# Attention: a tile's normalization issued ahead of the next tile's scores on VectorE, and the adaLN slabs spread otherwise over the rounds

## The chip, the cores and the metric

One core of one Trainium2 chip. The time is the device time of one execution in microseconds (us), from the first to the last instruction of the program with what lies around them; several executions are timed and the median is given. The trace is of one execution taken by the hardware profiler. Engines: PE is TensorE (PEld its weight loads), ACT ScalarE, DVE VectorE, POOL GpSimd, SP the engine that issues the transfers. Each runs its own instructions in the order in which the program issues them, and waits for others by semaphores.

## The reference

Two trunk layers over 128 context tokens and 512 latent tokens, width 1024, in float32. Each layer: half a SwiGLU, a mixer, half a SwiGLU, each behind an RMS norm that is scaled and shifted by vectors from the condition ("adaLN": nine vectors of 1024 for each layer, `silu(cond) @ w_ada + b_ada`). The mixer of layer 0 is what matters here:

```
proj = h @ w_in ; q, k, v, xb, gb = split(proj)
q = rms_norm(q) / 8 ; k = rms_norm(k)                  # over each head's 64 channels
latent: s = [q . k(8 x 16 neighbourhood) + bias | q . k_cached]   # 8 heads
context: s = q . k
p = softmax(s) ; o = p . v
y = concat(o, rglru(xb, gb)) @ w_out ; x = x + gate * y
```

## The kernel before, in words

Channels lie on the 128 partitions, tokens along the free dimension: 640 tokens in two halves of 320. Every float32 product is made of three passes over a high and a low part of each operand, so every weight, 128 x 1024 at a time (512 KB), is loaded, copied to its high part on ScalarE (`whi`, L176), and its low part is subtracted (`wlo`, L181), here on GpSimd while the attention runs.

The work is written out by hand in program order, with `manual_schedule`; nothing is reordered. What decides the order around the change:

- **The load list.** `add_w` and `add_slab` append weights and slabs to one list, `self.loads`. A *slab* is one 128 x 1024 piece of `w_ada`; eight of them make an adaLN vector. `load()` (its transfer is L139, on SP) takes the head of the list whenever a load buffer is free in program order, and stops where none is. Weights and slabs of the mixer share three load buffers, `self.buffers(self.const, None, 3, 5)`: three for loads (`st`), five pairs for split weights (`whi`, `wlo`). For the mixer's end the list holds the output weight `w_out_ab` number 0, then slabs up to 79, then `w_out_ab` 1 to 7.
- **`fill(n)`** uses n slabs: eight small matmul records each (`ada`, L327), then the slab's buffer is free and `load()` is called. After the eighth slab of a vector ScalarE evacuates the sums (`adaev`), and at the next vector's first slab `ada_end` turns them (`adaT`) and adds the bias on VectorE.
- **`prep(upto, 1)`** first calls `flush()`, which issues the low part of a weight begun earlier and frees its load buffer, then `load()`, then issues at most one new split (the high part), if that weight's load has been issued.

```
def split_later(self, it, hi, lo, src, then=None):
    self.nc.scalar.activation(out=hi, in_=src, func=AF.Copy)
    self.lows.append((it, hi, lo, src, then))     # low part and free_raw come with the next flush
```

The attention works on 20 tiles: four channel groups c of two heads, and for each five tiles j of 128 queries (j = 0 to 3 latent with 384 keys, j = 4 context with 128). It is a software pipeline over 23 rounds s:

- `A(s)`: scores on TensorE (`S`, L1262), bias and minimum on VectorE from PSUM (two instructions, L1268), two exponentials with their sums on ScalarE (L1271);
- `N(s)`: reciprocal of the sums and two scalings of the exponentials on VectorE (L1277, L1279);
- `B(s)`: transposes on TensorE (`PT`, L1288) and one copy out on ScalarE (`pt`, L1291);
- `C(s)`: products with v on TensorE (`o`, `op`, L1301); after j = 3 and j = 4 the high part on ScalarE (`hh`, L1307) and the low part on VectorE (`hl`, L1308).

Where a group begins, `vtr` transposes v (`vT`, L1243). GpSimd prepares the next group's bias (`nb`, L1233) as the tiles before it let go of the old one. A round before the change is B(s-2), one slab, A(s) with these, N(s-1), a piece of other work in the first rounds (`early`), one slab, C(s-3), `prep`. 36 slabs (44 to 79) are left when the attention begins, three of them loaded.

After the attention comes the output projection (`out_last`, its sums `pd`), which needs the adaLN vector of the gate, and uses `w_out_ab` 0 to 7 in order.

Of the kernel before, what the change touches and what calls it, by code (L numbers as in the profile page):

```python
# [13 lines left out]
PSUM = bass.MemoryType.PSUM  # L14

P = 128
# [16 lines left out]
class Item:  # L33
    """weights of one product: their loads, the steps that split them, what the steps made"""
# [7 lines left out]
class Kern:  # L42
# [21 lines left out]
    def buffers(self, pool, phase, n_st, n_w):  # L64
        """buffers for weights: as loaded, and split; those of a phase serve its weights only"""
        for j in range(n_st):
            self.st_free.append((pool.tile([P, 1024], F32, name=f"st{j}"), phase))
        for j in range(n_w):
            self.w_free.append((pool.tile([P, 1024], F32R, name=f"whi{j}"),
                                pool.tile([P, 1024], F32R, name=f"wlo{j}"), phase))  # L70
# [14 lines left out]
    def slab_pool(self, st, upto, bufs=2):  # L85
        """weights of the adaLN vectors: slabs up to this one are used in the phase"""
        self.slab_p = st.enter_context(self.tc.tile_pool(name="slab", bufs=bufs))
        self.s_dma = self.s_use
        self.s_end, self.s_bufs = upto, bufs

    def psum(self, pairs):
        """PSUM of a phase: six single banks or three pairs"""
        if self.ps_pairs is pairs:
            return
        self.ps_st.close()
        self.ps_pairs = pairs
        ps = self.ps_st.enter_context(self.tc.tile_pool(name="ps", bufs=3 if pairs else 6, space=PSUM))
        if pairs:
            self.pair = lambda name: ps.tile([P, 2, 512], F32, tag="mm", name=name)
            self.bank = lambda name: self.pair(name)[:, 0, :]  # L100
        else:
            self.bank = lambda name: ps.tile([P, 512], F32, tag="mm", name=name)
# [48 lines left out]
    def prep(self, upto, most=99):  # L151
        """steps for the items up to this one, as far as there are buffers"""
        self.flush()
        self.load()
        while self.steps and most:
            it, fn, need = self.steps[0]
            if it.idx >= min(upto, self.limit) or len(it.raw) < len(it.src) and fn in (self.split_w, self.quad_a, self.fold_a):
                return
            w = None
            if need:  # L160
                w = self.pick(self.w_free if need == 1 else self.s1_free, it.slots)
                if w is None:
                    return
            self.steps.pop(0)
            self.flush()
            fn(it, w)
            most -= 1
            self.load()
# [5 lines left out]
    def split_later(self, it, hi, lo, src, then=None):  # L174
        """the low part comes with the next step"""
        self.nc.scalar.activation(out=hi, in_=src, func=AF.Copy)  # L176
        self.lows.append((it, hi, lo, src, then))
# [18 lines left out]
    def fold_a(self, it, w):  # L196
        """rows m and -m: sum and difference"""
# [12 lines left out]
    # a pair of units as a 2 x 2 matrix (unit, half of the rows): the seven left factors of Strassen and Winograd  # L210
# [59 lines left out]
    def done(self, most=99):  # L270
        """the oldest unit in use is no longer needed"""
# [3 lines left out]
    def mm3(self, out, w, ks, xs, first=True, last=True):  # L275
        """out (+)= W^T X in three passes; w: (hi, lo) as [P, k, 128], xs: k -> (hi, lo)"""
# [8 lines left out]
    def mm_side(self, outs, ws, h, lag=0):  # L285
        """products of several units with half h, chunk after chunk as the norm gives them; the last two unit by unit
        lag: chunks by which the last unit stays behind"""
# [57 lines left out]
    def ada_end(self):  # L345
        """the finished vector, channels on partitions"""
# [28 lines left out]
    def parts(self, h):  # L375
        """pieces of a token half with one condition: (column slice, condition)"""
# [20 lines left out]
    def norm_s(self, h, bank=None):  # L397
        """sums of squares, tokens on partitions"""
# [6 lines left out]
    def norm_a(self, h):  # L405
        """rsqrt(mean(x^2) + eps)"""
# [4 lines left out]
    def rsqrt(self, ps, n=3):  # L411
        """rsqrt(mean(x^2) + eps) of n columns of sums"""
# [3 lines left out]
        # the exponent halved on the bits, then Newton's steps  # L416
# [21 lines left out]
    def T_pool(self, ks=range(4)):  # L438
        """right factors of Strassen and Winograd beside the parts of h"""
# [9 lines left out]
    def norm_r(self):  # L449
        """the factors of the tokens on all partitions"""  # L450
# [6 lines left out]
    def norm_high(self, h, l, i, c, r, keep):  # L457
        """h = rms_norm(x) g (1 + scale) + shift and its high part
        keep: for the products of a SwiGLU"""
# [24 lines left out]
    def direct(self, l, i, h, c, keep):  # L484
        """the high part comes without the sum of product and shift"""
# [19 lines left out]
    def norm_steps(self, h, l, i, keep=False):  # L505
        """a step for each chunk, low parts one step behind"""
# [17 lines left out]
    def t_sums(self, k, b12, b22):  # L524
        """T1 = B12 - B11, T2 = B22 - T1, T3 = B22 - B12, T4 = B21 - T2"""
# [21 lines left out]
    # slabs of a SwiGLU: after chunks of the first units, and after each quad  # L547
# [5 lines left out]
    def plan_ffn(self, l, n, s):  # L553
        """weights of a SwiGLU in the order of their use; s: the first slab, returns the next"""
# [36 lines left out]
    def ffn(self, l, i, after, mid=iter(()), late=None):  # L591
        """after(h, c): what follows the last update of chunk c, half h; mid: steps of other work, one in each quad;
        late: what follows the last quad"""
# [14 lines left out]
    def ffn_start(self, evac):  # L608
        """the first products of all: the first two vectors of adaLN come chunk by chunk, the norm and the products follow"""
# [7 lines left out]
        def ada(c):  # L617
            """the vectors' values for a chunk, four sums in groups of columns"""
# [178 lines left out]
    def down_last(self, fs, gate, after):  # L797
        """the last product before a norm: half 0 is through while four chunks of half 1 remain
        the first sums wait for the last chunk of the inner width"""
# [20 lines left out]
    def quad(self, f, fills, begin=False):  # L820
        """gate and up of a chunk, both halves of the tokens, in seven products
        M1 = A11 B11, M2 = A12 B21, M3 = S4 B22, M4 = A22 T4, M5 = S1 T1, M6 = S2 T2, M7 = S3 T3;
        C11 = M1 + M2, U2 = M1 + M6, C12 = U2 + M5 + M3, C21 = U2 + M7 + M4, C22 = U2 + M7 + M5"""
# [73 lines left out]
    def out_last(self, xs, gate, after):  # L897
        """the last product before a norm: half 0 is through while four chunks of half 1 remain"""
# [32 lines left out]
    def mix_setup(self):  # L931
        """parameters of the mixer, log_sigmoid(lambda)"""
# [13 lines left out]
        # y = |lam|, w = exp(-y) by halving steps and a series  # L946
# [17 lines left out]
        # log1p(w) = 2 artanh(w / (2 + w))  # L964
# [11 lines left out]
        # -2 log_sigmoid = 2 (2 artanh) - 2 min(lam, 0)  # L976
# [24 lines left out]
    def lru(self, c, xc, gel):  # L1001
        nc, lp = self.nc, self.lp
        n = 644
# [19 lines left out]
        for d in range(2):  # L1023
            # exp(-z) and t = tanh(z / 2): 1 - a = t (1 + a), 1 - a^2 = t (1 + a)^2
# [28 lines left out]
    def qk_norm(self, which, c, ps):  # L1053
        """RMS norm over each head's 64 channels; q also gets -1/8"""
# [47 lines left out]
    def mixer0(self, after):  # L1102
        nc, tc = self.nc, self.tc
        self.bg, self.fg = [], []
        with ExitStack() as st:
# [18 lines left out]
            with ExitStack() as s2:  # L1124
# [60 lines left out]
                def early():  # L1185
                    """work that the first tiles of the attention cover"""
# [41 lines left out]
    def bias(self, c, v):  # L1228
        """mask less position bias of a variant of the windows' columns"""
# [6 lines left out]
    def attention(self, early):  # L1236
# [82 lines left out]
        n = len(tiles)  # L1319
        for s in range(n + 3):  # L1320
            if 0 <= s - 2 < n:
                B(*tiles[s - 2])
            self.fill(min(1, 80 - self.s_use))
# [12 lines left out]
            if 0 <= s - 1 < n:  # L1336
                N(*tiles[s - 1])
            next(early, None)
            self.fill(min(1, 80 - self.s_use))
# [12 lines left out]
    def fourier_const(self):  # L1352
        """the DFT matrices in the place of the right factors, a step for each piece"""
# [18 lines left out]
        def steps():  # L1372
# [9 lines left out]
            # the shift times the root of the number of tokens, by chunk in the group, group, condition  # L1382
# [10 lines left out]
    def scaled(self, h, c):  # L1393
        """x g (1 + scale) in parts; the factors of the tokens follow the channels' transform"""
# [12 lines left out]
    def fourier_front(self, const):  # L1407
        """what follows the updates before the transform"""
# [25 lines left out]
    def tok_rest(self):  # L1434
        """factors of the other tokens; the third tile has the end of half 0 and the start of half 1"""
# [8 lines left out]
    def fourier(self, after):  # L1444
        nc, tc = self.nc, self.tc
        NP, NQ, MP, MQ = self.NP, self.NQ, self.MP, self.MQ
        with ExitStack() as st:
# [6 lines left out]
            with ExitStack() as s2:  # L1454
# [11 lines left out]
                def chan(k, g):  # L1466
                    """the channels' transform: token tile k, group g"""
# [9 lines left out]
                def chan_out(k, g):  # L1477
                    """times the factors of the tokens, in parts"""
# [26 lines left out]
                # the shift's part, the same for all tokens  # L1505
# [25 lines left out]
                def pos(r):  # L1531
                    """rows r: cosines of group r, 4 the Nyquist channels, 5 + g sines of group g"""
# [9 lines left out]
                    def shift(q):  # L1542
                        """the shift stays at the first position"""
# [18 lines left out]
            with ExitStack() as s2:  # L1562
# [14 lines left out]
                for c in range(KD):  # L1577
# [17 lines left out]
                    # token n has the sum, the one as far from the end the difference  # L1595
# [16 lines left out]
    def run(self, stop=99):  # L1612
        nc, a = self.nc, self.a
        const = self.const
        with self.tc.manual_schedule():
# [29 lines left out]
            for n in range(KD):  # L1645
                if n == 1:
                    for i in range(s, 80):
                        self.add_slab(i, None)
# [21 lines left out]
            def after(l, i, first=4, per=3, keep=True):  # L1670
                """the next norm: half 0 while the last products of half 1 run"""
# [49 lines left out]
def pack(inp):  # L1721
    """lays the inputs out; no arithmetic"""
# [9 lines left out]
    # the first two vectors by chunks of channels  # L1732
# [47 lines left out]
    # DFT matrices: channels (columns: cosines 0..127, the first halved, cosine 128, sines 1..127) and positions  # L1780
# [37 lines left out]
```

## Time and profile before

| | us |
|---|---|
| median of 3 runs | 2305.5 (2305.37 to 2310.3) |
| span of the profiled execution | 2305.0 |
| busy in it: PE / DVE / ACT / POOL | 2224.0 / 1554.8 / 990.7 / 954.9 |
| first slab of the attention to its end, 689.06 to 778.50 | 89.44 |
| busy there: PE / DVE / ACT / POOL | 72.44 / 46.46 / 53.77 / 29.35 |

The profile gives no time of its own for the profiled execution beside its span. Rows of the timeline give start, duration, engine, line, operation, tiles written and read with their shapes and the count of merged instructions; in brackets stand the idle time before it and who ended it. Rows of the chain of waits give start, duration and what the end waited for at that moment. The busy time of PE is the union of modelled spans, so it is not the same as PE at its peak.

### The profile page before, as it was taken

To read this page: it belongs to the slowest core of one execution; us is meant where nothing else is said; L and a number is where in the kernel's file an instruction comes from. 1 tells how busy PE (TensorE), PEld (TensorE's weight loads), DVE (VectorE), ACT (ScalarE), POOL (GpSimd) and SP (SyncE) were. 2 spreads that over 40 slices of the span, in tenths; PEclk is the share of its full clock that TensorE was granted. 3 is DMA by queue.
4 is the path that set the end of the run, shared out by engine and by line. 5 is a ranking of instruction groups with operands and counts; after the bars stand their busy time and mean duration, and the time that the engine had idled before them with its cause. 6 is when DMAs were issued, how large, how long until landed. Compare 5 with 4: busy or idle time off the path is not lost.

```text
span 2305.0 us, 39901 instructions
## 1 busy us (share of the span) xinstructions
PE 2224.0 (96%) x15534; PEld 2110.0 (92%) x15534; DVE 1554.8 (67%) x2871; ACT 990.7 (43%) x1780; POOL 954.9 (41%) x856
## 2 busy tenths in 40 slices
PE   7999999999998899999999999999999989999999
PEld 5889999999994788999999889999999979999999
DVE  6676677666865368666666786666667786666665
ACT  4433333347855435333333453333335553333332
POOL 2444444440023235444444454444443645444441
PEclk9999999999999999999999999999999999999999
DMA  7333333321228424333322243332332322222221
GB/s 278 113 111 105 105 107 107 115 74 56 73 71 267 131 83 137 110 101 110 106 91 97 75 155 120 110 97 96 103 117 62 128 85 83 83 83 83 83 89 57
DMA packets 75316, 245.44 MB, mean 106 GB/s; under 512 B 8756, under 2 KB 12996, under 8 KB 75128
## 3 DMA queue, kind: packets, MB, share of 16 engines
q1 hardware_dynamic: 74168, 241.28, 31.7%
q8 instruction: 123, 2.02, 0.4%
q10 hardware_dynamic: 864, 1.38, 0.2%
q14 instruction: 65, 0.53, 0.1%
q0 software_dynamic: 96, 0.22, 0.0%
HBM read 239.71 MB, written 3.15 MB: 105 GB/s over the span
## 4 chain that ended last, share of the span: by engine, by line
PE 79%; DVE 13%; ACT 4%; issue 2%; POOL 2%; DMA 1%; ACTq 0%; DVEq 0%; SPq 0%; POOLq 0%
PE q L282 40%; PE pd L282 26%; PE pj L282 5%; DVE wlo L181 2%; PE ada L327 2%; DVE tl L172 1%; PE pg L282 1%; PE gt L1014 1%; PE pos L1549 1%; DVE x L381 1%; PE S L1262 1%; DVE y L473 1%; DVE sx L1268 1%; PE PT L1288 1%; DMA st<-w_ada 1%
## 5 line engine op out<-in xcount | busy, mean ns | idle before, releaser
L181 DVE TENSOR_TENSOR wlo<-st,whi 128x1024 fp32r<-128x1024 f32 (+2 forms) x401 | 498.4, 1254 | 11.1 <-ACT whi L176 10.2
L176 ACT ACTIVATE whi<-st 128x1024 fp32r<-128x1024 f32 (+2 forms) x405 | 401.2, 992 | 233.0 <-POOL st L232 139.3
L282 PE MATMUL pd<-g,whi 128*128 128x320 f32 x1536 | 347.0, 310 | 4.3 <-DVE u L825 2.3
L381 DVE SCALAR_TENSOR_TENSOR x<-pd,mods,x 128x128 f32<-128x128 f32 (+2 forms) x696 | 265.0, 433 | 111.7 <-PE pd L282 111.2
L282 PE MATMUL q<-hh,wlo 128*128 128x320 f32 x960 | 296.9, 309 | 5.3 <-DVE wlo L181 5.3
L282 PE MATMUL q<-hh,whi 128*128 128x320 f32 x960 | 300.7, 313 | 1.0 <-DVE u L825 1.0
L282 PE MATMUL q<-th,whi 128*128 128x320 f32 x960 | 297.3, 310 | 3.0 <-DVE sg L825 3.0
L282 PE MATMUL q<-tl,whi 128*128 128x320 f32 x960 | 296.6, 309 | 0.7 <-POOL tl L172 0.7
L282 PE MATMUL q<-th,wlo 128*128 128x320 f32 x960 | 296.6, 309 | 0.0
L282 PE MATMUL q<-hl,whi 128*128 128x320 f32 x960 | 296.3, 309 | 0.0
L231 POOL TENSOR_TENSOR st<-sums,st 128x512 f32<-128x512 f32 x80 | 118.0, 1474 | 396.9 <-DVE wlo L181 359.5
L825 POOL TENSOR_TENSOR u<-u,u 128x320 f32<-128x320 f32 x80 | 106.5, 1331 | 401.0 <-DVE u L825 401.0
L282 PEld LDWEIGHTS pd<-g,whi 128*128 128x128 f32 x1536 | 256.8, 188 | 8.9 <-DVE x L381 3.1
L282 PE MATMUL pd<-hh,whi 128*128 128x320 f32 x768 | 238.4, 310 | 0.0
L282 PE MATMUL pd<-hl,whi 128*128 128x320 f32 x768 | 237.9, 310 | 0.0
L282 PE MATMUL pd<-g,wlo 128*128 128x320 f32 x768 | 237.7, 310 | 0.0
L282 PE MATMUL pd<-hh,wlo 128*128 128x320 f32 x768 | 236.8, 308 | 0.0
L826 ACT ACTIVATE sg<-sg 128x320 f32<-128x320 f32 x160 | 75.4, 471 | 284.5 <-DVE sg L825 284.5
L282 PEld LDWEIGHTS q<-hh,whi 128*128 128x128 f32 x960 | 180.2, 188 | 16.8 <-issue 8.6
L282 PEld LDWEIGHTS q<-th,whi 128*128 128x128 f32 x960 | 180.3, 188 | 6.6 <-issue 4.7
L282 PEld LDWEIGHTS q<-hh,wlo 128*128 128x128 f32 x960 | 180.2, 188 | 6.4 <-DVE wlo L181 6.4
L282 PEld LDWEIGHTS q<-tl,whi 128*128 128x128 f32 x960 | 180.4, 188 | 1.5 <-POOL tl L172 1.5
(327 smaller groups left out, 5016.0 us busy)
## 6 DMA issues: line engine op xcount, KB each, us to landing
st<-w_ada SPq DMA_DIRECT2D x144, 512.0 KB, 4.6
st<-ffn_gate SPq DMA_DIRECT2D x88, 512.0 KB, 3.6
st<-ffn_up SPq DMA_DIRECT2D x88, 512.0 KB, 3.7
st<-ffn_down SPq DMA_DIRECT2D x96, 384.0 KB, 3.1
st<-w_in SPq DMA_DIRECT2D x20, 512.0 KB, 3.5
st<-ffn_down SPq DMA_DIRECT2D x16, 512.0 KB, 3.5
st<-w_out_ab SPq DMA_DIRECT2D x8, 512.0 KB, 3.5
st<-w_out_c SPq DMA_DIRECT2D x8, 512.0 KB, 3.5
```

Of the source, the lines that this page charges most:

```text
L172: (eng or self.nc.vector).tensor_tensor(out=lo, in0=src, in1=hi.bitcast(F32), op=ALU.subtract)
L176: self.nc.scalar.activation(out=hi, in_=src, func=AF.Copy)
L181: self.low.tensor_tensor(out=lo, in0=src, in1=hi.bitcast(F32), op=ALU.subtract)
L231: self.nc.gpsimd.tensor_tensor(out=s[:, 0:512], in0=it.s1, in1=s[:, 0:512], op=ALU.subtract)
L282: self.nc.tensor.matmul(out, lhsT=l, rhs=r, start=first and j == 0, stop=last and j == len(ops) - 1)
L327: nc.tensor.matmul(self.ada_ps[32 * j:32 * j + 32, 0:256], lhsT=self.s_sb[:, k, :], rhs=t[:, 256 * j:256 * j + 256], start=k == 0, stop=k ...
L381: self.nc.vector.scalar_tensor_tensor(out=self.x[h][c][:, sl], in0=ps[:, sl], scalar=gate[:, c, r:r + 1], in1=self.x[h][c][:, sl], op0=ALU ...
L473: nc.vector.tensor_tensor(out=y, in0=self.x[h][c], in1=r, op=ALU.mult)
L825: tt = lambda e, o, a, b, op=ALU.add: e.tensor_tensor(out=o, in0=a, in1=b, op=op)
L826: cp = lambda o, p, fn=AF.Copy: nc.scalar.activation(out=o, in_=p, func=fn)
L1014: nc.tensor.matmul(g[:, s, 0:322], lhsT=wt[:, d, j, :], rhs=xc[:, 322 * s:322 * s + 322], start=True, stop=True)
L1262: nc.tensor.matmul(o, lhsT=q, rhs=k, start=True, stop=True)
```

## The change

N(s-1) is issued ahead of A(s) and what goes with it, instead of behind. The number of slabs of a round is read from a list instead of being two: 3, 2, 2 in rounds 0 to 2, one in rounds 3 to 16 (in the second place, behind A), two in 17 to 19 and three in 20 to 22; the smaller half of a round's count goes ahead of N and A. In the load list the last nine slabs (71 to 79) move from ahead of `w_out_ab` 1 to behind `w_out_ab` 3. Everything else in the diff is comment strings.

```
+        fills = [3, 2, 2] + [1] * 14 + [2] * 3 + [3] * 3
+        assert sum(fills) == 80 - self.s_use
         for s in range(n + 3):
             if 0 <= s - 2 < n:
                 B(*tiles[s - 2])
-            self.fill(min(1, 80 - self.s_use))
+            self.fill(fills[s] // 2)
+            if 0 <= s - 1 < n:
+                N(*tiles[s - 1])
             if s < n:
                 c, j = tiles[s]
                 if j == 0:
...
                     if j == 3:
                         self.cache_load(c + 1)
-            if 0 <= s - 1 < n:
-                N(*tiles[s - 1])
             next(early, None)
-            self.fill(min(1, 80 - self.s_use))
+            self.fill(fills[s] - fills[s] // 2)
             if 0 <= s - 3 < n:
                 C(*tiles[s - 3])
             self.prep(self.n_use + 5, 1)
...
             for n in range(KD):
-                if n == 1:
-                    for i in range(s, 80):
-                        self.add_slab(i, None)
+                for i in {1: range(s, 71), 4: range(71, 80)}.get(n, ()):
+                    self.add_slab(i, None)
                 self.add_w(self.a["w_out_ab"][n], 1024)
```

More of the change, by code (lines that the diff above doesn't have):

```diff
@@ L1319, in attention @@
         n = len(tiles)
+        fills = [3, 2, 2] + [1] * 14 + [2] * 3 + [3] * 3
+        assert sum(fills) == 80 - self.s_use
         for s in range(n + 3):
@@ L1322, in attention @@
                 B(*tiles[s - 2])
-            self.fill(min(1, 80 - self.s_use))
+            self.fill(fills[s] // 2)
+            if 0 <= s - 1 < n:
+                N(*tiles[s - 1])
             if s < n:
@@ L1335, in attention @@
                         self.cache_load(c + 1)
-            if 0 <= s - 1 < n:
-                N(*tiles[s - 1])
             next(early, None)
-            self.fill(min(1, 80 - self.s_use))
+            self.fill(fills[s] - fills[s] // 2)
             if 0 <= s - 3 < n:
@@ L1645, in run @@
             for n in range(KD):
-                if n == 1:
-                    for i in range(s, 80):
-                        self.add_slab(i, None)
+                for i in {1: range(s, 71), 4: range(71, 80)}.get(n, ()):
+                    self.add_slab(i, None)
                 self.add_w(self.a["w_out_ab"][n], 1024)
```

## Prediction, made before the changed kernel was run

> **What bounds the kernel now.** I read the page first: one span, one chain that runs mostly through TensorE. Then the chain of waits over the attention stage, because the edit touches nothing else.
>
> ```profile
> span 2305.0 us, 39901 instructions
> PE 79%; DVE 13%; ACT 4%; issue 2%; POOL 2%; DMA 1%; ACTq 0%; DVEq 0%; SPq 0%; POOLq 0%
> ```
>
> ```profile
> 715.44 0.56 DVE sx L1268
> 716.01 0.47 DVE sx L1268
> 716.48 0.09 DVE z L1277
> 716.60 0.43 DVE sx L1279
> 717.03 0.14 issue
> 717.16 0.84 PE PT L1288 x6
> 718.01 0.57 PE ada L327 x8
> 718.58 0.88 PE S L1262 x8
> 719.48 0.56 DVE sx L1268
> ...
> 731.04 0.70 PE vT L1243 x5
> ...
> 758.14 4.64 DMA st<-w_out_ab
> ...
> 778.75 45.76 PE pd L282 x312
> ```
>
> The first nine lines are one whole round, 4.04 us: VectorE's two reductions A(s) (L1268), then the normalization N(s-1) (L1277, L1279), TensorE's transposes B(s-1) that wait for it, a slab, the scores S(s+1), and the next reductions. Every link but the slab waits for the one before it, so neither engine is full. The line at 758.14 is a weight load on which ScalarE stood at the end. At 778.5 the attention is over, and from there TensorE runs 45.76 us without a break: what the attention gains or loses, the kernel gains or loses. The profiled execution's span, 2305.0, is 0.5 below the median of the runs, 2305.5; my differences are made in the trace and set on 2305.5. This kernel's measurement can tell about 0.2% (4.6 us) from no change.
>
> **Part 1: N(s-1) ahead of A(s).** No instruction is added. On VectorE the 2 reductions, one reciprocal and 2 scalings of a round change places. B(s) then no longer waits for the reductions of the next tile, but A(s), queued behind N(s-1), now waits for ScalarE's exponentials of s-1. The new ring is A(s), exp(s), N(s), A(s+1).
>
> ```profile
> 716.10 0.61 ACT L1271 ACTIVATE sx<-sx,m 128x384 f32<-128x384 f32 x1 [2.45 <-DVE m L1268]
> ...
> 716.60 0.75 DVE L1279 TENSOR_SCALAR sx<-sx,z 128x384 f32<-128x384 f32 x2
> ...
> 717.32 0.41 ACT L1307 ACTIVATE hh<-o 128x320 fp32r<-128x320 f32 x1
> ...
> 718.65 0.36 DVE L1308 TENSOR_TENSOR hl<-o,hh 128x192 fp32r<-128x192 f32 x1 [0.40 <-ACT hh L1307]
> ...
> 720.19 1.52 POOL L1233 TENSOR_TENSOR nb<-mk,u 128x256 f32<-128x256 f32 x2 [3.42 <-DVE m L1268]
> ...
> 720.63 1.29 DVE L1279 TENSOR_SCALAR sx<-sx,z 128x384 f32<-128x384 f32 x2
> ```
>
> Exponentials start 0.66 after the reductions (715.44 to 716.10) and take 1.22 (to 717.32): 1.88. N adds about 1.0: 0.05 of handover, 0.20 for the reciprocal, 0.75 for two undisturbed scalings (716.60); beside POOL's bias work they took 1.29. The five tiles of a channel group then give, from one A to the next:
> - j=0: 1.88 + 1.0 = 2.88.
> - j=1: the outputs of the group before come between; from the exponentials' end at 717.32 to the end of the second hl at 719.01 is 1.69. 1.88 + 1.69 + 1.0 = 4.57.
> - j=2: a small output, some 0.57 by the same two steps at a third of the width: 3.45.
> - j=3: POOL's bias work starts as the reductions end (1.03) and holds the scalings until 2.55; 0.75 more: 3.30.
> - j=4: short on VectorE, but now TensorE is late: B 0.84, six v transposes 0.81, S 0.88, handover 0.20: 2.73.
>
> Sum 16.9 for five rounds, 3.39 each, against the 21.2 that five rounds take now (15 in the first row below, 63.3). TensorE's other duties fit in: a plain round is B 0.84, S 0.88, one slab 0.57, output C some 0.8, so 3.1.
>
> ```profile
> 701.29:764.61 63.32, 54.64 (x603) 32.87 (x599) 32.67 (x118) 34.45 (x89) 15.26 (x21) 1.00 0.82 263
> ```
>
> This stretch goes from S(3) to S(18), the columns being length, then PE, PEld, DVE, ACT, POOL busy, granted clock, DMA share, GB/s. PE is busy 54.64 in it; 12 slabs of 0.57 leave it, so 47.8 is the floor for these 15 rounds. My ring gives 3 x 16.9 = 50.8. The ends: 47.8 if TensorE sets the pace, 63.3 if nothing shortens.
>
> **Part 2: the slabs, first and middle rounds.** Before, two slabs a round for 18 rounds, 36 in all; after, 3, 2, 2, then one a round for 14, then 2, 2, 2, 3, 3, 3. Slabs pass through three load buffers, refilled as TensorE lets go.
>
> ```profile
> 693.59 0.64 PE L327 MATMUL ada<-st,s_sb 128*32 128x256 f32 x8 [0.38 <-DMA st<-w_ada]
> ```
>
> The fourth slab is there at 693.59 in either version; after the change it stands ahead of S(1), which slips by 1.9 us. One slab fewer in round 3 and the earlier N give it back, so I let S(3) start at 701.3 as now (estimate, plus or minus 1), and A(3) 0.9 later. A(18) is then at 702.2 + 50.8 = 753.0 and S(18) begins, as worked out below, at 751.2 instead of 764.61: some 13 us gained so far.
>
> **Part 3: the last nine slabs and three weights.** The load list becomes 27 slabs, weights w1, w2, w3, nine slabs, w4 to w7. On SP's queue w1 to w3 pass ahead of nine slab loads; on ScalarE and POOL the splits of w1 to w3 stand in rounds 18, 19, 20 (before: 16, 17, 18). A load can be put on the queue only when a buffer is free in program order. w1 gets the buffer of the 25th slab (second fill of round 18), w2 and w3 those of the 26th and 27th (round 19). After that all three buffers hold weights. One weight is split per round, and its buffer comes free only with the flush at the end of the next round. So round 20, which wants three slabs, has one buffer: slab 28 is loaded once w1's low part is done, 29 once TensorE has used 28, 30 once it has used 29; the same buffer serves 31, 33 and 35. w2's buffer returns only at the end of round 20, w3's after round 21. Six loads stand in line, each begun when the one before is consumed.
>
> ```profile
> 762.80 1.06 ACT L176 ACTIVATE whi<-st 128x1024 fp32r<-128x1024 f32 x1 [1.97 <-DMA st<-w_out_ab]
> ...
> 763.94 2.35 POOL L181 TENSOR_TENSOR wlo<-st,whi 128x1024 fp32r<-128x1024 f32 x1 [16.45 <-ACT whi L176]
> ```
>
> ```profile
> st<-w_out_ab SPq DMA_DIRECT2D x3, 512.0 KB, 3.5
> ```
>
> ```profile
> st<-w_ada SPq DMA_DIRECT2D x21, 512.0 KB, 4.5
> ```
>
> A load that has the queue to itself lands in 3.5 (window 766 to 775), with two or three in flight in 4.5 (712 to 757). From issue of w1 to the end of its low part took 758.14 to 766.29, 8.15. Behind ScalarE's wait for w1 stand pt(17) and exp(19), wanted by nobody before the slab line is through.
>
> ```profile
> 767.44:770.85 3.41, 0.93 (x8) 0.66 (x8) 2.63 (x5) 2.52 (x6) 2.93 (x2) 0.95 0.57 163
> 770.85:774.27 3.42, 3.42 (x25) 2.70 (x24) 1.92 (x10) 2.64 (x6) 1.83 (x2) 0.55 0.53 171
> 774.27:777.68 3.41, 2.24 (x31) 1.66 (x30) 0.49 (x1) 1.99 (x5) 2.07 (x1) 1.00 0.47 133
> ```
>
> ```profile
> 46.04 1.24 PE L624 MATMUL ada<-st,s_sb 128*32 128x256 f32 x12
> ```
>
> After a stretch with 0.93 of 3.41 busy the granted clock (third column from the end) fell to 0.55 for the next one and came back after a full stretch. In the slab line TensorE works well under 1 us in every 4, so I take the half clock there: eight slab matmuls cost 1.24 x 8/12 = 0.83 instead of 0.57. A step is 3.5 + 0.83 + 0.1 of handover = 4.4.
>
> The sum: the second fill of round 18 ends 0.3 before A(18), at 752.7 (that round's S ends about 0.9 ahead of A, because TensorE needs only N(16) for it, so S begins at 751.2; the slab takes 0.57); w1's low part is done at 760.8. Six steps make 26.6. Loads 31, 33 and 35 each have a neighbour in flight: 3 x 0.7 to 1.0, so 2.5. The 36th slab's matmuls 0.8, the last output C with its hh and hl 1.3, adaT 0.4: 31.6. The products that follow start at half clock; 3.4 to 6.8 us until it is back, at nearly half speed, lose about 2. 760.8 + 31.6 + 2 = 794.4 against 778.5: 15.9 us lost. 2305.5 + 15.9 = 2321.4, call it 2321. The other edits (comment strings) issue nothing.
>
> A price from a page: the Trainium skill, "DMA: Bandwidth & Descriptors", section "Anatomy of one DMA", fits a transfer as about 2.0 us fixed plus its bytes at 436 GB/s, measured on the other issue path. An estimate for 512 KB is 3.2 us, and the sum would be some 2 us lower, 2319; the row's 3.5 decides.
>
> **The rivals.**
> *The slabs are hidden (faster).* If three or more buffers were free in rounds 20 to 22, the end would come as now, 13.9 us after S(18) (764.61 to 778.5), plus the twelve slabs that are then still to do, at 0.57: 751.2 + 13.9 + 6.8 = 771.9, 6.6 us faster, 2299. For it: now 36 slabs pass three buffers at about 2 us each without much waiting. Against it: two of three buffers hold w2 and w3 in round 20. It decides if no more than two of the six loads stand alone in line (15.9 / 4.4 = 3.6 steps make the difference).
> *The new ring gains nothing (slower still).* If waits for POOL or for ScalarE's evacuations hold N, the 15 rounds stay at 63.3: 12.5 us more, 2334. For it: N may meet POOL in each of 3 rounds of 5, and 1.29 was seen. Against it: all of my rounds but j=1 would have to grow by a third.
> *The clock stays up in the slab line.* Then eight slab groups save 0.26 each, and the restart about 2: 2317. The row above speaks against it. The Trainium skill, "TensorE: Matmul & The Clock Gate", section "Part 1", gives half clock as the state after at least one idle window of some 3.4 us; read strictly, a window with a slab in it is not idle. The trace disagrees with that reading: 0.93 busy was followed by 0.55.
> *The parts cancel.* Fewer steps in line (three or four) and a ring near the floor: within 4.6 us of 2305.5.
>
> **How the numbers follow.** Forecast with half clock 0.55, clock up 0.20: both slower by over 0.2%. No gain in the ring 0.10. Parts cancel 0.08. Slabs hidden 0.07. Slower 0.85, same 0.08, faster 0.07. The likeliest gives 2321. Its own bounds: TensorE's floor takes off 3, the clock 4, shorter loads 2, so 2312; loads at 4.5 instead of 3.5 add 6, rounds a little longer 4, so 2331. The range 2311 to 2331 leaves out the hidden slabs and most of the ring without gain.
>
> **What would show it.** Part 1 right: in the middle rounds A to A falls from 4.2 to about 3.4, TensorE's wait for sx (L1279) nearly goes, and VectorE waits for ScalarE at L1277. Part 3 right: slab loads 28, 29 and 30 issued one after another, each behind TensorE's ada; TensorE waits for w_ada for some 20 us in all near the end of the attention; clock near 0.5 there. Wrong: loads in pairs or threes, or pd starting before 778.

## The result, and the profile after

| | before | after |
|---|---|---|
| median of 5 runs, us | 2307.45 (2305.37 to 2310.30) | 2318.84 (2317.89 to 2324.74) |
| span of the profiled execution, us | 2305.0 | 2317.6 (its own time 2319.41) |
| first output sum `pd` of the mixer begins (its weight load, in the trace) | 778.47 | 792.22 |
| `nst`, the first step of the norm behind it, in the chain of waits | 824.51 | 839.83 |

The ratio is 1.0057, interval 1.0046 to 1.0068, so slower and clear of noise. The two medians are 11.4 us apart, the ratio stands for some 13 us; the text below goes by the medians. The median of before in the table ahead of the prediction, 2305.5, is that of the first three of these five runs. The prediction said 2321, between 2311 and 2331, slower.

The chain of waits over the end of the attention, after the change (start, duration, what the end waited for):

```profile
751.76 0.85 PE S L1262 x8
...
753.29 4.42 DMA st<-w_out_ab
757.74 1.07 ACT whi L176
...
758.87 2.37 POOL wlo L181
761.25 3.47 DMA st<-w_ada
...
764.76 1.12 PE ada L327 x8
765.90 3.32 DMA st<-w_ada
...
770.49 3.56 DMA st<-w_ada
...
775.24 3.52 DMA st<-w_ada
...
779.94 3.55 DMA st<-w_ada
...
784.67 0.33 SPq L139
...
785.05 4.45 DMA st<-w_ada
...
789.54 1.08 PE ada L327 x8
790.62 0.65 PE op L1301 x4
...
792.64 47.19 PE pd L282 x312
839.83 1.25 PE nst L402 x12
```

S(18) starts at 751.76, some 13 us earlier than the 764.61 of before: the first half of the change gives what it was reckoned at. Then the chain is one line for 37 us: the load of w1 (753.29), its high part, its low part on GpSimd (to 761.25), and six of the nine slab loads, each issued when TensorE has used up the slab before it (the sixth right behind a load of another buffer, the `SPq` row). The first three have the queue to themselves; beside the others a load for one of the other two buffers is under way. Before, the same place had the one load of w1, and `pd` followed 14 us after S(18); now it follows 40 us after. From `pd` on the work is that of before, with 47.19 us instead of 45.76.

Two rounds of the middle on VectorE in the timeline after (starts of the reductions `sx<-S`, L1268, mark a round):

```profile
717.44 0.55 DVE L1268 CUSTOM_DVE_ANT_0 sx<-S,nb 128x384 f32<-128x384 f32 x1
...
720.93 0.55 DVE L1268 CUSTOM_DVE_ANT_0 sx<-S,nb 128x384 f32<-128x384 f32 x1
...
722.92 0.17 DVE L1277 RECIPROCAL z<-z 128x2 f32<-128x2 f32 x1 [0.87 <-ACT sx L1271]
723.12 0.75 DVE L1279 TENSOR_SCALAR sx<-sx,z 128x384 f32<-128x384 f32 x2
723.79 0.28 DVE L1268 CUSTOM_DVE_ANT_0 sx<-S,nb 128x128 f32<-128x128 f32 x1
```

The rounds take 3.49 and 2.86 us. The order is the new one, reductions, exponentials, scalings, next reductions, and the reciprocal waits for ScalarE (0.87). The waits from 689 to 797 (engine, line, whom it waited for: total, times, longest), after:

```profile
PEld ada L327 <- DMA st<-w_ada: 24.6, 13, 6.3
PE ada L327 <- DMA st<-w_ada: 20.5, 12, 6.0
DVE z L1277 <- ACT sx L1271: 15.1, 14, 3.5
DVE sx L1268 <- PE S L1262: 5.2, 6, 1.3
PE PT L1288 <- DVE sx L1279: 2.5, 3, 1.2
```

and the same waits before:

```profile
DVE sx L1268 <- PE S L1262: 29.7, 19, 3.1
PE PT L1288 <- DVE sx L1279: 13.8, 19, 3.6
PEld ada L327 <- DMA st<-w_ada: 1.4, 3, 0.6
```

The waits between TensorE and VectorE fell from 43.5 to 7.7 us, and waits for `w_ada` that hardly existed took their place. TensorE's waits for `w_ada`, 20.5 us, are the "some 20" of the prediction. Stretches of after (length, busy PE, PEld, DVE, ACT, POOL, granted clock, DMA share, GB/s): the rounds from A(3), at 702.99, to just ahead of A(18), at 753.45, and the slab line.

```profile
702.96:753.29 50.33, 46.27 (x507) 30.94 (x504) 31.21 (x118) 34.07 (x92) 14.98 (x20) 1.00 0.58 194
761.50:795.70 34.20, 18.30 (x119) 8.77 (x120) 1.67 (x7) 4.49 (x9) 4.54 (x2) 0.50 0.57 194
```

15 rounds now take 50.5 us, at full clock; from A(3) to A(18) it was 64.2 before (12.6 to 76.8 after the first `vT`). In the slab line the clock is at half throughout. The transfers moved 194 GB/s in both stretches: in the first the work went on beside them, in the second it waited for each.

### The profile page after: what moved, and what is told of

Its sections match the earlier page's. It is cut to its first block, busy times and chain, and to the rows that moved or that the text cites. A ratio compares the mean times of both kernels' runs of the same rounds, so it can differ in the third digit from the quotient of the medians.

```text
span 2317.6 us, 39901 instructions
## 1 busy us (share of the span) xinstructions
PE 2234.5 (96%) x15534; PEld 2118.7 (91%) x15534; DVE 1552.8 (67%) x2872; ACT 990.2 (43%) x1780; POOL 955.0 (41%) x855
## 4 chain that ended last, share of the span: by engine, by line
PE 80%; DVE 11%; ACT 4%; issue 2%; DMA 2%; POOL 1%; ACTq 0%; SPq 0%; DVEq 0%; POOLq 0%
PE q L282 41%; PE pd L282 27%; PE pj L282 5%; PE ada L327 2%; DVE wlo L181 2%; DVE tl L172 1%; DMA st<-w_ada 1%; PE pg L282 1%; PE gt L1014 1%; PE pos L1552 1%; DVE x L381 1%; DVE y L473 1%; ACT hh L481 1%; DVE hl L495 0%; PE nst L402 0%
## 5 line engine op out<-in xcount | busy, mean ns | idle before, releaser
L181 DVE TENSOR_TENSOR wlo<-st,whi 128x1024 fp32r<-128x1024 f32 (+3 forms) x402 | 499.1, 1252 | 11.6 <-ACT whi L176 11.0
L381 DVE SCALAR_TENSOR_TENSOR x<-pd,mods,x 128x128 f32<-128x128 f32 (+2 forms) x696 | 265.1, 432 | 112.2 <-PE pd L282 111.8
```

What stands on the lines that cost most here:

```text
L181: self.low.tensor_tensor(out=lo, in0=src, in1=hi.bitcast(F32), op=ALU.subtract)
L381: self.nc.vector.scalar_tensor_tensor(out=self.x[h][c][:, sl], in0=ps[:, sl], scalar=gate[:, c, r:r + 1], in1=self.x[h][c][:, sl], op0=ALU ...
```

## The experiments

Two theories. T1: N first and one slab a round gain some 13 us, and the new load list loses more, since w1 to w3 hold two of the three load buffers when the last slabs are wanted, so that slab loads go one at a time. The rival T2: the list is harmless, and the loss comes from leaving 15 slabs to the last six rounds, that is from the spread. A further rival for part 1: N first gains nothing by itself. Each experiment was timed in five rounds beside the kernel before on the same chip; differences below are to that (medians 2306.99, 2307.08 and 2306.80 in the three groups of runs, the changed kernel to its own 2307.45). All of them compute the whole reference.

### N first alone

```
-        fills = [3, 2, 2] + [1] * 14 + [2] * 3 + [3] * 3
+        fills = [2] * 18 + [0] * 5
-                for i in {1: range(s, 71), 4: range(71, 80)}.get(n, ()):
+                for i in {1: range(s, 80)}.get(n, ()):
```

> Only the order on VectorE is changed: N(s-1) ahead of A(s); two slabs a round for 18 rounds and the load list stay as before. Theory (the loss comes from the line of slab loads behind w1 to w3, N first is a gain): a round falls from 4.24 us to what TensorE needs with two slabs, 3.7 to 3.8, so 8 us faster than before, about 2299. Rival (N first itself costs, since A then waits for the exponentials of the tile before): not faster than 2307, or slower.

Measured 2302.24, ratio 0.9982 (0.9973 to 0.9990): 4.8 us faster, the sign that T1 gives, but less than expected. The waits from 689 to 772 show one reason:

```profile
PEld ada L327 <- DMA st<-w_ada: 7.1, 14, 1.2
```

Before, with 4.3 us a round (64.2 for 15), this row was 1.4 us in 3 waits. Here 15 rounds take 60.4 us, 4.0 each, and not the 3.4 that the new order reaches with one slab a round: two slabs do not arrive in that time (some 2.1 us each, as the run with the old list below shows), and the second one takes TensorE's time too. A second reason lies behind the attention: the clock is at half for 6.8 us from 770.7 on, and from the first `pd` to `nst` it takes 48.2 us instead of 45.7. Part 1 needs a lower rate of slabs to pay in full.

### The spread alone, N in its old place, old load list

```
-            if 0 <= s - 1 < n:
-                N(*tiles[s - 1])
             if s < n:
...
+            if 0 <= s - 1 < n:
+                N(*tiles[s - 1])
             next(early, None)
-                for i in {1: range(s, 71), 4: range(71, 80)}.get(n, ()):
+                for i in {1: range(s, 80)}.get(n, ()):
```

> Only the new counts of slabs (3, 2, 2, one in 14 rounds, 2, 2, 2, 3, 3, 3); N behind A and the load list as before (all slabs ahead of w1). Theory: the old ring without the slab in its middle is 3.5 a round, 10 us gained up to round 17; then 12 slabs are left that the transfers bring at some 1.9 us each, which gives most of it back: 2303 to 2306. Rival (three slabs in each of the last rounds cost by themselves): slower than 2307.

Measured 2312.99, ratio 1.0025 (1.0015 to 1.0036): 6.0 us slower; the expectation missed, and the rival in it was right. A plain round did fall to 3.47, but the rounds with outputs did not fall as far, and A(18) came only 7.0 us earlier, counted from the first `vT` (69.8 instead of 76.8). The rest is in its chain, where the last slabs are used up faster than they arrive:

```profile
763.79 4.50 DMA st<-w_ada
...
774.92 4.33 DMA st<-w_ada
```

The clock was at half for 13.7 us there, and from the first `pd` to `nst` it took 49.8 us instead of 45.7. So T2 holds a part of the truth: the spread by itself costs.

### N first and the spread, old load list

```
-                for i in {1: range(s, 71), 4: range(71, 80)}.get(n, ()):
+                for i in {1: range(s, 80)}.get(n, ()):
```

> The changed kernel with the load list of before: all slabs ahead of w1. Theory: no line of single loads, three buffers stay with the slabs; S(18) as in the changed kernel, then the last slabs come at 1.9 us each: 4 us faster than before, 2303, and 15 faster than the changed kernel. Rivals (N first costs, or three slabs a round at the end cost): slower than 2307 still.

Measured 2305.82, ratio 0.9997 (0.9988 to 1.0006): no difference from before, and 12.6 us better than with the new list (11.4 + 1.2). This is one line of the change undone, and it returns the whole loss: T1 against T2. It is 3 short of the expectation, for the end is still bound by transfers, now three in flight:

```profile
752.85 4.47 DMA st<-w_ada
...
769.42 4.84 DMA st<-w_ada
...
776.71 8.09 PE pd L282 x48
...
785.49 1.14 DVE wlo L181
```

Ten slab loads are issued between 752.85 and 769.42 and have landed by 774.3, so 2.1 us a slab with two or three in flight, against some 4.7 a slab in the line of the changed kernel. The last line is new: after 48 of the `pd` records TensorE waits for w1's low part, which VectorE makes behind its first residual updates (L381).

### The spread and the new list, N in its old place

The edit of the spread alone, with the load list of the changed kernel.

> The changed kernel with N behind A, as before: new counts and new load list alone. Theory: the same line of six single loads, reached a little later if the old ring is slower: 2319 to 2323. Rival (N first costs): faster than the changed kernel by what N costs, 2312 or less.

Measured 2328.67, ratio 1.0095 (1.0081 to 1.0109): 21.7 us slower; the sign was expected, the size was not. The first `pd` comes 110.5 us after the first `vT`, in the changed kernel 101.7. Together the five kernels give each part its price, by what else is there:

| | without the other parts | with the spread | with spread and list |
|---|---|---|---|
| N first | -4.8 | -7.2 | -10.3 |

The spread costs 6.0 with N in its old place and 3.6 with N first (6.0 - 7.2 + 4.8); the list costs 15.7 with N old (21.7 - 6.0) and 12.6 with N first. The parts are not additive: N first pays more with one slab a round than with two. Why it pays 3 us more again beside the new list stays open.

### Only one weight ahead of the last nine slabs

```
-                for i in {1: range(s, 71), 4: range(71, 80)}.get(n, ()):
+                for i in {1: range(s, 71), 2: range(71, 80)}.get(n, ()):
```

> The changed kernel with one weight (w1) ahead of the last nine slabs instead of three. Theory: two buffers are left to the slabs from round 19 on and the third returns at its end, so loads overlap as with the load list of before: 2304 to 2307, some 13 us under the changed kernel, not a third of the loss taken away but nearly all. Rival (each weight ahead costs its own wait and split): about two thirds of the loss gone, 2310.

Measured 2308.35, ratio 1.0005 (0.9996 to 1.0013). With no weight ahead the difference to before is -1.2, with one +1.3, with three +11.4. So 10 of the 12.6 us that the list costs are gone, between the "nearly all" of the theory and the two thirds of the rival; the time alone does not decide between them. The trace does: w1's load and its split are still in the chain (752.65 to 760.61), but two buffers stay with the slabs, their loads run two and three at a time, and the chain holds three of them (3.59, 4.46 and 4.90 us) where the changed kernel has six. What costs is how many of the three buffers the weights hold.

### Low part and next loads in the same round

```
             self.prep(self.n_use + 5, 1)
+            self.flush()
+            self.load()
```

> The changed kernel, with the low part of a weight issued, and its load buffer freed, at the end of the same attention round instead of at the end of the next. Theory (the buffers that w1 to w3 hold make the line of single loads): w2's buffer returns one round sooner, round 20 has two buffers, loads 29 to 36 run two and three abreast; the last slab is used some 7 us sooner and the time is 2311 to 2313. Rival (three slabs a round at the end, or the transfer rate, set the tail): 2317 to 2320 as the changed kernel.

Measured 2316.97, ratio 1.0044 (1.0031 to 1.0057). Missed: the time is that of the rival, and the interval overlaps that of the changed kernel. Its chain:

```profile
757.68 2.36 POOL wlo L181
760.05 3.63 DMA st<-w_out_ab
...
764.84 2.36 POOL wlo L181
767.21 0.33 SPq L139
```

The buffer that w1 gives back earlier goes to the head of the list, and that is w2: its load starts only when w1's low part is done (760.05), and the second of the nine slabs takes w2's buffer and waits for w2's low part in turn (767.21). Loads on SP's queue go in order, so all later ones stand behind it. The loss has only been moved: two loads and splits of weights in line, in place of some of the six slabs. Freeing a buffer earlier did not help while the weights stood ahead in the list.

### The changed kernel with TensorE kept busy in the slab line

```
+        def fill(s, k):
+            for _ in range(k):
+                m = {71: 40, 72: 18, 73: 18, 74: 18, 76: 18, 78: 18}.get(self.s_use, 0)
+                if m:
+                    w = self.bank("wk")
+                    for _ in range(m):
+                        nc.tensor.transpose(w[:, 0:128], self.ident, self.ident)
+                self.fill(1)
```

It adds transposes whose result nobody uses, ahead of the slabs that are loaded alone.

> The changed kernel with TensorE kept busy while it waits in the slab line: 18 transposes of the identity (2.5 us, results unused) ahead of each slab that is loaded alone, 40 ahead of the first. Theory (besides the six loads, the half clock costs): the slab matmuls return from 1.1 to 0.6 us, the products after the attention start at full clock: six times 0.5 and 1.4, some 4 to 5 us under the changed kernel, 2313 to 2315. Rival (only the loads in line cost, the clock nothing): 2317 to 2320.

Measured 2317.80, ratio 1.0049 (1.0037 to 1.0062): missed. The time is that of the rival, and the interval overlaps that of the changed kernel, so no gain is shown by the time. Its trace, from the slowest of its runs (2321.64), does show what the clock is worth in the line itself:

```profile
772.29 0.67 PE ada L327 x8
772.98 3.57 DMA st<-w_ada
...
793.79 45.76 PE pd L282 x312
```

and the clock of the line (a stretch, with the granted clock in the third column from the end):

```profile
764.40:793.60 29.20, 20.30 (x210) 14.41 (x207) 2.88 (x7) 4.35 (x9) 4.80 (x3) 1.00 0.60 191
```

The slab matmuls take 0.67 instead of 1.12, a step 4.2 to 4.5 instead of 4.7, and `pd` runs its 45.76 at full clock. That is about 3 us less from A(19) to the norm (34.4 + 45.7 against 35.9 + 47.3). In the same execution 6.8 us of half clock fell into the middle rounds, where the traces of before and after have none, and A(19) came 3.7 later, counted from the first `vT`:

```profile
719.20:726.00 6.80, 6.43 (x42) 3.91 (x43) 3.35 (x15) 3.52 (x10) 1.84 (x3) 0.50 0.24 80
```

The added transposes stand far behind that place, and the next kernel, without them, has such a stretch of 3.4 us at 718.2 too. Both follow a lull: TensorE was busy for 1.35 of the 3.40 us ahead of the one (715.8 to 719.2) and for 1.53 ahead of the other, while in the middle rounds of before and after no 3.4 us have less than 2.31 and 1.77. Why the lulls fell there stays open, and with it how much of the 3 us the kernel could have kept.

### Slabs evenly, or more of them in front (N first, old list)

```
-        fills = [3, 2, 2] + [1] * 14 + [2] * 3 + [3] * 3
+        fills = [2, 1] * 11 + [3]                      # evenly
+        fills = [2] * 11 + [1] * 11 + [3]              # in front
```

> N ahead of A, the load list of before, and slabs spread evenly: 2, 1 in turn for 22 rounds, 3 in the last. Theory: with N first a round needs about 3.2 us on VectorE and ScalarE, and TensorE has room for 1.5 slabs in it; the transfers keep up, no slab is left for a line at the end: 2295 to 2299. Rival (the transfers or the end bind whatever the spread): 2302 or more, as N first alone.

> As the even spread, but two slabs a round in rounds 0 to 10, one in 11 to 21, three in the last. Theory: the first half runs at the rate of the transfers (two slabs in 3.8 us or more), the second half at the ring's 3.2, and all three buffers are full before the last round: 2296 to 2300, within 2 us of the even spread. Rival (the end binds): 2302 or more.

Measured 2302.22, ratio 0.9980 (0.9971 to 0.9989), and 2305.10, ratio 0.9991 (0.9982 to 1.0000): faster than before or the same, and both in the range of their rival (2302 or more) and not in that of the theory. With more slabs in front single rounds of the first half go up to 5.0 to 5.5 us; what sets these is not shown. Evenly spread, the rounds are good (A(19) 69.3 after the first `vT`, before 82.0), but the gain shrinks from the 12.7 there to 3.6 at the norm. Its chain:

```profile
764.92 4.49 DMA st<-w_ada
...
772.55 8.77 PE pd L282 x48
...
782.02 1.14 DVE wlo L181
```

The last slab of the last round is waited for in an otherwise empty stretch, the clock falls to half, `pd` starts slowly, and then it waits for w1's low part. These two are what the last two kernels go after.

### The slabs through a round earlier, and w1's split finished in the last round

```
-        fills = [3, 2, 2] + [1] * 14 + [2] * 3 + [3] * 3
+        fills = [2, 2, 1] * 7 + [1, 0]                 # the other: [2, 2, 1] * 4 + [2, 1] * 5 + [1]
...
-            self.prep(self.n_use + 5, 1)
+            if s == n + 2:
+                self.prep(self.n_use + 5, 1)
+                self.flush()
...
-                for i in {1: range(s, 71), 4: range(71, 80)}.get(n, ()):
+                for i in {1: range(s, 80)}.get(n, ()):
```

N first, old list. No weight is split in rounds 0 to 21; w1's split comes in the last, and its low part goes out with it on GpSimd instead of with the next flush, behind the attention. In the first of the two no slab is left to the last round, in the second one is.

> N ahead of A, load list of before, slabs 2, 2, 1 in turn so that the last is used in round 21, and the split of w1 held back to the last round, with its low part on GpSimd there. Theory: no load stands in line, ScalarE waits for no weight inside the rounds, w1 is ready when the output product wants it: 3 to 5 us under the even spread, 2297 to 2300. Rival (the transfers bind at five slabs in three rounds): 2302 or more.

> As the last, with 2, 2, 1 for 12 rounds, then 2, 1 for 10 and one in the last. Theory: 2297 to 2300, within 1.5 us of the other. Rival (the last slab is again a line at the end): 2302 as the even spread.

Measured 2291.97, ratio 0.9934 (0.9921 to 0.9948), and 2292.80, ratio 0.9941 (0.9929 to 0.9954): both beat both kernels by more than the expectation, 14.8 us less than before and about 27 less than the changed kernel. The chain of the first:

```profile
753.50 4.33 DMA st<-w_ada
...
765.79 45.76 PE pd L282 x312
```

One load is waited for at the end, with work behind it; `pd` starts 13.0 us earlier than in the chain of before (778.75) and runs without a break at full clock. A(19) is at 69.0, as with the even spread (69.3); the difference of 8.9 us at the norm (122.1 against 131.0 after the first `vT`) arises behind it. By the traces 4.9 of it lies ahead of the first `pd`, where the even spread waits for its last slab, and 3.7 behind, where its `pd` starts at half clock and TensorE stops for 1.6 (ahead of 783.2) on w1's low part. The last slabs and w1's split were not tried apart; the two counts of slabs make no difference that can be told.

## Why the prediction was right, point by point

**The ring of part 1** held. A to A was predicted at 2.88, 4.57, 3.45, 3.30, 2.73 for j = 0 to 4; in the trace after, the groups from A(5) on have 2.87 to 3.34, 4.32 to 4.33, 3.22 to 3.48, 2.86, and 2.47 to 3.31 at the same five places (the first group, with the slip of its start in it, ends with 4.45 and 2.34). Predicted for 15 rounds 50.8, measured 50.5 (five rounds of before are 21.1 by the row, not 21.2; nothing hangs on it); S(18) at 751.2, measured 751.76, of which 0.87 is that the attention began later in this trace (first `vT` 690.50 instead of 689.63). n_alone adds that this needs the lower slab rate.

**The first rounds** (part 2): the slip was spread otherwise, two rounds of 3.9 instead of one of 5.0, but A(3) came 12.5 after the first `vT`, before 12.6, as assumed. That the two agree so well is in part luck: in three other kernels that run the same program up to there (the old list, one weight ahead, the added transposes) it came 13.3 to 13.8 after.

**The line of six loads** (part 3) is there with its cause, order and count: w1 issued at 753.29 (predicted 752.7), its low part done at 761.25 (760.8), six loads behind one another, `pd` at 792.22 (792.4 by the same sum without the restart). Two terms in it were off and cancel. The slab matmuls took 1.12, not 0.83: the row of twelve records that the 0.83 was scaled from straddles the end of a half clock, as the stretch of before that holds it shows (granted clock in the third column from the end):

```profile
46.04:47.28 1.24, 1.24 (x17) 0.52 (x16) 0.92 (x2) 0.26 (x1) 1.24 (x2) 0.67 0.00 0
```

So five steps took 23.4 (761.25 to 784.67), 4.7 each, where 4.4 was reckoned. And the neighbours in flight cost less: of the three loads that had one only the last landed late (4.45), and the rest of the line, from 784.67 to 790.62, took 5.95, that is 1.3 above a plain step, where 2.5 for neighbours and 0.8 for the 36th slab had been set. The slow restart cost 1.4 (47.19 - 45.76), predicted 2.

**The size of the loss** came out smaller, 11.4 by the medians (some 13 by the ratio) against 15.9. The 2321 was set on 2305.5; on the median of the five runs of before, 2307.45, the same loss makes 2323. So it is partly luck that the forecast is only 2 us from the measured time. In the trace the norm is 15.3 us late (839.83 against 824.51), of which 0.87 arose ahead of the attention; so the stage itself lost 14.4, 1.5 less than reckoned, by small differences in S(18), the line and the restart. But the span is only 12.6 longer. The larger term that was missing lies behind the stage that the prediction looked at. Chain before:

```profile
852.52 1.81 PE nbc L453 x6
854.33 8.61 PE pg L282 x42
...
881.68 1.09 DVE hl L495
```

Chain after:

```profile
867.98 1.06 PE nbc L453 x6
...
894.56 1.08 DVE hl L495
```

Until `nbc` the delay is 15.46, at `hl` 12.88. Both traces have half clock near there, as the granted clock of these stretches shows (of before, then of after):

```profile
852.40:859.20 6.80, 6.68 (x24) 6.37 (x25) 4.16 (x11) 2.94 (x6) 1.75 (x2) 0.50 0.03 12
857.10:863.90 6.80, 6.80 (x30) 6.80 (x30) 5.91 (x8) 2.24 (x4) 5.38 (x4) 0.50 0.54 184
```

Before, it falls on the products `pg`, which hold the chain for 8.61. After, it falls on an earlier piece of the work, a norm that waits for VectorE, and `pg` is no longer in the chain. No edit touches this part of the program, and from `nst` to the end of the span the thirteen traces take between 1478.0 and 1480.7 us, the changed kernel the least and the kernel before the most. "What the attention gains or loses, the kernel gains or loses" was the step that failed, by 2.6 us. The remaining 1.2 lies between one pair of traced executions and the medians.

**The rivals.** *The slabs are hidden* was to decide if no more than two of the six loads stand alone: six stood in line, three of them with the queue to themselves. *The ring gains nothing* fell in the trace and by n_alone. *The clock stays up* fell: 0.50 through 34 us; and the kernel with added transposes shows some 3 us of the 4 reckoned in that stage of its trace, though not in its time. *The parts cancel* needed three or four steps in line; with one weight ahead, where the chain has three slab loads, they do (ratio 1.0005). The strict reading of the Trainium skill, "TensorE: Matmul & The Clock Gate", "Part 1", by which half clock follows only a window without any work, is not what this trace shows either: the half clock at 857.1 follows 3.40 us in which TensorE was busy for 1.52. The slab line itself does not test it. There the clock fell at 761.5, when TensorE had stood still since 758.7, in the wait for w1 and its split; and in the prediction's row with 0.93 of 3.41 busy it fell at 770.5, after a pause from 766.3 to 769.9. What the line does show is that the clock stayed down: from 764.76 to 784.67 TensorE was busy for 9.33 of 19.91 us (the slabs and the outputs between them) and had 0.50 all the time, until `pd` had filled 3.4 us. The estimate of 3.2 us for a lone transfer by the Trainium skill, "DMA: Bandwidth & Descriptors", "Anatomy of one DMA", stood against 3.47, 3.32 and 3.56 for the three that had the queue to themselves; the row's 3.5 was nearer than the fit.

## What to carry to other kernels

Before a stream is reordered, count the buffers that it has in program order at each point: a weight that has landed and waits for its low part is a buffer less for the stream behind it, and with one buffer left a load costs its full latency each time. The stage in which a stream is consumed should match the rate at which it can arrive; slots that are freed (here by N first) pay only as far as the transfers follow. And a wait for a transfer in a queue in program order (a split on ScalarE, a load on SP behind a late buffer) is best put where the queue has nothing else to do; the last two kernels did this, together with an earlier end of the slabs, and the two were not tried apart.

## What the runs showed of the hardware that was not expected

- The half clock did not end while TensorE was busy for about half of the time, 9.33 of 19.91 us in the slab line: 0.50 from 761.5 to 795.7. In the kernel with added transposes 20.3 us busy of 29.2 kept it at 1.00 over the same line. No full pause is needed for it to begin: in the thirteen traces every stretch of half clock inside the program follows 3.41 us in which TensorE was busy for anything from 0 to 2.62, and ends with 3.41 us in which it was busy for 2.86 or more.
- Stretches of half clock come and go in steps of about 3.4 us (3.4, 6.8, 10.2, 13.7, 23.9, 34.1), at times that shift against the work from kernel to kernel. One 6.8 us stretch cost 2.6 us more on TensorE's products than on a norm that waits for VectorE. Differences below some 3 us between two traces should be looked for there first.
- Eight slab matmuls take 0.57 at full clock behind other matmuls, 0.61 to 0.68 beside a wait, 1.08 to 1.13 at half clock.
